# Residual and conv tiles loaded several products earlier, and the Strassen pair operands made in two steps instead of four

## The chip, the cores and the metric

The kernel runs as one program on one core of a Trainium2 chip. The metric is the device time of one execution in microseconds (us); three runs of the kernel before gave 2842.70, 2845.52 and 2847.58 us, so the median is 2845.52 us. TensorE (PE) multiplies; its weight loads are shown as PEld. VectorE (DVE), ScalarE (ACT) and GpSimd (POOL) do the elementwise work, and SyncE (SP) and POOL issue DMAs. Each engine runs its own list of instructions strictly in order, so an instruction that waits holds everything behind it on that engine.

## The reference

One layer of a decoder on 512 prompt tokens and 32 sample tokens (NT = 544 columns, held as two halves of 272):

```
proj = rmsnorm(x) @ w_in               # 2048 -> SSD group + conv group
y = rmsnorm(ssd(...) * silu(z))        # 2048 channels
u = silu(layernorm(dwconv31(...)))     # 2048 channels, the "conv half"
x = x + concat([y, u]) @ w_out         # 4096 -> 2048, the out-projection
g, v = split(dwconv3(rmsnorm(x) @ w_up))
x = x + (silu(g) * v) @ w_down         # 2048 -> 2*5504 -> 2048
return rmsnorm(x), states...
```

All of it is in float32. The kernel keeps activations transposed (channels on the 128 partitions, tokens along the row), splits every operand of a matrix product into a rounded high part and a low rest, and computes high*high + high*low + low*high, three matmuls for each 128x128 block of weights.

## The kernel before, in words

The y half of the out-projection is done early by the jobs "oy"; its result goes to DRAM (tiles `xrd`). The change lies in what follows, a stream of "products" (`items`), which one loop at the end of the function walks. Three stretches of it matter:

- **Group stage.** Eight Groups (one for output tiles t and t+8) take ten of the sixteen u tiles, with a Strassen-like scheme: seven products of five blocks each (15 matmuls) instead of eight. A Group reads five weight tiles `wr`; two of them are sums of two weight blocks, which are made by a plain load (SP, L1180) and a second load that accumulates onto it (POOL, L1182). The buffers are five in number, so the tile of the next Group is loaded when the same tile of this Group has been used up. DVE makes the sum `ws` of several of them (L1192, L1196).
- **Plain stage.** Sixteen Plain products (36 matmuls each) take the last six u tiles (`Uh`, `Ul`), one output tile each, in the order 0, 8, 1, 9, ...
- **Up stage.** 43 Groups of the up-projection, seven products of eight blocks (24 matmuls), in pairs of operands `T_t`.

Before a product can run, ACT rounds its weights (`sh`, L1205) and DVE makes the rest (`sl`, L1214), both two products ahead. After it, `evac` adds the PSUM result into the residual tile `xres`: L1253 to L1266 in the group stage, L1300 in the Plain stage. The loop makes, for product q: the ACT part for q+2, the evac of q-1, the tasks hung on q with `at_item`, the DVE part for q+2, the sums, and then the matmuls. So all of these stand in this order on DVE's and ACT's lists.

The residual tile of an output tile is x (load L1073 on SP, from `in_xT`) plus the y half (L1076 on POOL, an accumulating load of `xrd`). The six u tiles of the Plain stage come back from DRAM (`ur`, L1274) and are split into `Uh` on ACT and `Ul` on DVE (L1106, L1107). In the Plain stage the evac also makes `xs` (ACT, L1302) and a square `sq` (L1304), which POOL adds up (L1308). From each two tiles xs[k], xs[k+8] `prep_pair` makes the seven operands of the up stage in four steps, `first`, the pair of q, `second` and `third`; each step is an ACT cast (`Ta`, `Th`) followed by a DVE subtraction (`Ta` low, `Tl`), and the last two begin with DVE differences `tr` (L1126, L1127, L1132, L1133).

Of the kernel before, what the change touches and what calls it, by code (L numbers as in the profile page):

```python
# [8 lines left out]
F32 = mybir.dt.float32  # L9
F32R = mybir.dt.float32r  # L10
AF = mybir.ActivationFunctionType
ALU = mybir.AluOpType
# [18 lines left out]
def hymba_step_kernel(ctx: ExitStack, tc: tile.TileContext, a: dict):  # L31
    nc = tc.nc
    V, G, S, T, Y = nc.vector, nc.gpsimd, nc.scalar, nc.tensor, nc.sync
# [24 lines left out]
    def nm(p):  # L58
        cnt[0] += 1
        return f"{p}{cnt[0]}"  # L60

    def slot(p, shape=None, dt=F32, side=False):
        return (Cur.side if side else slots).tile(shape or [128, 2, NH], dt, tag="s", name=nm(p))
# [14 lines left out]
    def flat(t):  # L78
        return t.rearrange("p h x -> p (h x)")
# [188 lines left out]
    with tc.manual_schedule():  # L268
        win, wout, wup, wdn = a["w_in"], a["w_out"], a["w_up"], a["w_down"]

        def in_srcs(t):
            return [(win[t, :, i * 512:(i + 1) * 512], 4) for i in range(4)]
# [14 lines left out]
        st = [in_srcs(j) for j in (J_XBC + 16, J_XBC + 20, J_DT)]  # L287
# [778 lines left out]
        xres, xs, T_t = {}, {}, {}  # L1066
# [4 lines left out]
        def load_xr(t):  # L1071
            xres[t] = slot("xres")
            Y.dma_start(out=flat(xres[t]), in_=a["xT"][t])  # L1073

        def add_xr(t):
            G.dma_start(out=flat(xres[t]), in_=xr_dram[t], accum_op=ALU.add)  # L1076
# [28 lines left out]
        def split_into(h, l, src):  # L1105
            S.copy(h, src)  # L1106
            V.tensor_tensor(l, src, h.bitcast(F32), ALU.subtract)  # L1107

        tr = {}

        def prep_pair(T, k, p, q):

            def pair(src, ms):
                h, l = slot("Th", dt=F32R), slot("Tl", dt=F32R)
                split_into(h, l, src)
                for i, m in enumerate(ms):
                    T[m, k] = (h[:, i, :], l[:, i, :])

            def first():
                t = slot("Ta", dt=F32R)  # L1120
                split_into(t[:, 0, :], t[:, 1, :], p()[:, 0, :])
                T[0, k] = (t[:, 0, :], t[:, 1, :])

            def second():
                r = tr[k] = slot("tr")
                V.tensor_tensor(r[:, 1, :], p()[:, 0, :], p()[:, 1, :], ALU.subtract)  # L1126
                V.scalar_tensor_tensor(r[:, 0, :], r[:, 1, :], -1.0, q()[:, 1, :], ALU.mult, ALU.subtract)  # L1127
                pair(r, (2, 3))

            def third():  # L1130
                r, s = tr.pop(k), slot("tr")
                V.tensor_tensor(s[:, 0, :], q()[:, 1, :], p()[:, 1, :], ALU.subtract)  # L1132
                V.scalar_tensor_tensor(s[:, 1, :], r[:, 0, :], -1.0, q()[:, 0, :], ALU.mult, ALU.subtract)  # L1133
                pair(s, (4, 6))
            return first, lambda: pair(q(), (1, 5)), second, third
# [15 lines left out]
        def at_item(q, fn):  # L1151
            tasks.setdefault(q, []).append(fn)
# [88 lines left out]
        def block_evac(t):  # L1241

            w = []

            def f(m, o):
                x, y = xres[t], xres[t + 8]
                if m == 0:
                    w[:] = [slot("pd")]
                p = w[0]
                if m == 0:  # L1250
                    S.copy(p[:, 0, :], o)
                elif m == 1:
                    V.tensor_tensor(x[:, 0, :], o, x[:, 0, :], ALU.add)  # L1253
                    V.tensor_tensor(x[:, 0, :], x[:, 0, :], p[:, 0, :], ALU.add)
                elif m == 2:
                    V.tensor_tensor(p[:, 0, :], o, p[:, 0, :], ALU.add)  # L1256
                elif m == 3:
                    V.tensor_tensor(p[:, 1, :], o, p[:, 0, :], ALU.add)
                    V.tensor_tensor(x[:, 1, :], x[:, 1, :], p[:, 1, :], ALU.add)
                elif m == 4:  # L1260
                    V.tensor_tensor(p, o.unsqueeze(1).to_broadcast([128, 2, NH]), p, ALU.add)
                    V.tensor_tensor(y, y, p, ALU.subtract)
                elif m == 5:
                    V.tensor_tensor(x[:, 1, :], o, x[:, 1, :], ALU.add)
                else:
                    V.scalar_tensor_tensor(y[:, 0, :], o, -1.0, y[:, 0, :], ALU.mult, ALU.add)  # L1266
            return f


        Uh, Ul, ur = {}, {}, {}  # L1270

        def u_load(t):
            ur[t] = slot("ur")
            Y.dma_start(out=flat(ur[t]), in_=un_dram[t])  # L1274

        def u_split(t):
            Uh[t], Ul[t] = slot("Uh", dt=F32R), slot("Ul", dt=F32R)
            split_into(Uh[t], Ul[t], ur.pop(t))

        for i in range(8):  # L1280
            lo, hi = (wout[t, :, 2048 + UP * 128:4096] for t in (i, i + 8))
            q = len(items)
            Group(lo, hi, NU, T_u, block_evac(i))
            if i:
                at_item(q - 5, lambda i=i: load_xr(i))
                at_item(q - 2, lambda i=i: add_xr(i))
                at_item(q - 2, lambda i=i: load_xr(i + 8))
                at_item(q + 1, lambda i=i: add_xr(i + 8))
        for t in range(UP):
            at_item(28 + 4 * t, lambda t=t: u_load(t))  # L1290
            at_item(30 + 4 * t, lambda t=t: u_split(t))

        def out_evac(i):
# [19 lines left out]
        q = len(items)  # L1313
        for i in range(16):
            Plain(wout[OT[i], :, 2048:2048 + UP * 128], UP, lambda k: (Uh[k], Ul[k]), out_evac(i))
        for k in range(8):
            st = prep_pair(T_t, k, lambda k=k: xs[k], lambda k=k: xs[k + 8])
            for f, d in zip(st, (2, 2, 3, 3)):
                at_item(q + 2 * k + d, f)
            at_item(q + 2 * k + 3, lambda k=k: (xs.pop(k), xs.pop(k + 8)))  # L1320

        fstate, fcw = [], None

# [138 lines left out]
        for c, (n, pn) in enumerate(DOWN):  # L1462
            q = len(items)
# [234 lines left out]
```

## Time and profile before

| | |
|---|---|
| median of three runs | 2845.52 us |
| the profiled execution: time, and its span from first to last instruction | 2846.82 us, 2845.1 us |
| PE busy, share of the span | 2779.6 us, 98% |
| DVE busy | 2161.8 us, 76% |
| ACT busy | 1234.5 us, 43% |
| POOL busy | 906.8 us, 32% |
| mean granted clock of TensorE over the span | 0.991 |
| chain of work that ended last, by engine | PE 47%, DVE 1% |

Busy time of PE counts overlapping, pipelined matmuls, so 98% does not mean that it runs at its peak: the number of matmuls in a stretch tells its pace. In the page's row of 40 slices (71 us each) PE shows 9 nearly everywhere, and 8 in the three slices from 1209 to 1423 us, which hold most of the stages named above. The waits of PE in the whole span add up to some 50 us. TensorE's clock is granted at one of two levels; a clock of 0.90 in a stretch means that it ran at the lower one for a fifth of it.

### The profile page before, as it was taken

The page shows a single profiled execution, that of the slowest core. Times are in us where ns is not written, and L with a number is a line of the kernel's source. Part 1 is how long each engine was busy: PE and PEld are TensorE (multiplying, and loading weights), DVE is VectorE, ACT ScalarE, POOL GpSimd, SP SyncE. Part 2 cuts the span into 40 slices and gives each one's busy share as a digit, 9 for nine tenths or more (in the row PEclk, how much of TensorE's full clock was granted, in tenths as well). Part 3 has the DMA queues.
Part 4 walks back from the last instruction along what each step waited for, and adds up shares of the span by engine and source line. Part 5 has one row for each costly group of instructions (what it writes and reads, how often), then busy time and mean ns, then how long its engine had stood idle before and what let it go on. Part 6 is the DMA issues. An engine that isn't in the chain of part 4 may idle for free. (4 is left out here: it accounts for less than half of the span.)

```text
span 2845.1 us, 55518 instructions
## 1 busy us (share of the span) xinstructions
PE 2779.6 (98%) x22094; PEld 2749.9 (97%) x22094; DVE 2161.8 (76%) x3314; ACT 1234.5 (43%) x1827; POOL 906.8 (32%) x938
## 2 busy tenths in 40 slices
PE   8999999999999999988899999999999999999997
PEld 8999999999999999988799999999999999999997
DVE  7576665777787776666788888888888887778775
ACT  6545444333333324334444444444444443344344
POOL 5567667667666644311200000000000000100103
PEclk9999999999999999999999999999999999999999
DMA  4243244333333344586467776777776776765761
GB/s 168 84 132 100 91 144 136 102 99 105 104 98 98 93 135 130 156 216 173 122 179 184 191 195 186 192 188 189 195 191 184 197 192 207 173 182 160 176 184 64
DMA packets 197252, 433.50 MB, mean 152 GB/s; under 512 B 38400, under 2 KB 43136, under 8 KB 196992
## 3 DMA queue, kind: packets, MB, share of 16 engines
q1 hardware_dynamic: 175392, 362.57, 40.7%
q0 software_dynamic: 21600, 67.38, 13.5%
q8 instruction: 173, 2.83, 0.4%
q14 instruction: 87, 0.71, 0.1%
HBM read 385.78 MB, written 44.08 MB: 151 GB/s over the span
## 5 line engine op out<-in xcount | busy, mean ns | idle before, releaser
L1233 PE MATMUL st<-Th,sl 128*128 128x272 f32 x2880 | 835.9, 290 | 18.4 <-DVE sl L1214 18.4
L1230 PE MATMUL st<-Th,sh 128*128 128x272 f32 x2880 | 834.6, 290 | 1.0 <-ACT sh L1205 1.0
L1231 PE MATMUL st<-Tl,sh 128*128 128x272 f32 x2880 | 833.8, 290 | 0.0
L119 POOL TENSOR_TENSOR wl<-raw,wh 128x512 fp32r<-128x512 f32 x336 | 447.6, 1336 | 424.5 <-ACT wh L118 366.4
L1205 ACT CAST sh<-wr 128x1024 fp32r<-128x1024 f32 (+3 forms) x399 | 369.1, 926 | 464.2 <-PE st L1231 349.6
L1233 PEld LDWEIGHTS st<-Th,sl 128*128 128x128 f32 x2880 | 545.0, 189 | 21.2 <-DVE sl L1214 21.2
L1230 PEld LDWEIGHTS st<-Th,sh 128*128 128x128 f32 x2880 | 545.3, 189 | 1.4 <-ACT sh L1205 1.4
L1231 PEld LDWEIGHTS st<-Tl,sh 128*128 128x128 f32 x2880 | 545.0, 189 | 0.0
L229 PE MATMUL mm<-xh,wh 128*128 128x272 f32 x2304 | 483.2, 291 | 7.3 <-ACT xh L313 7.3
L229 PE MATMUL mm<-xl,wh 128*128 128x272 f32 x2304 | 479.2, 289 | 1.4 <-DVE xl L315 1.4
L229 PE MATMUL mm<-xh,wl 128*128 128x272 f32 x2304 | 478.5, 289 | 0.0
L1214 DVE TENSOR_TENSOR sl<-wr,sh 128x1024 fp32r<-128x1024 f32 (+3 forms) x399 | 427.4, 1071 | 56.0 <-ACT sh L1205 55.9
L118 ACT CAST wh<-raw 128x512 fp32r<-128x512 f32 x352 | 216.0, 616 | 433.6 <-PE mm L229 335.2
L229 PEld LDWEIGHTS mm<-xh,wh 128*128 128x128 f32 x2304 | 368.0, 188 | 16.0 <-ACT xh L313 7.3
L229 PEld LDWEIGHTS mm<-xl,wh 128*128 128x128 f32 x2304 | 365.5, 188 | 2.4 <-DVE xl L315 2.4
L229 PEld LDWEIGHTS mm<-xh,wl 128*128 128x128 f32 x2304 | 365.2, 188 | 0.0
L1182 POOL DMA_DIRECT2D wr<-in_w_up x86 | 74.9, 871 | 836.0 <-DVE pu L1348 390.7
L940 DVE SCALAR_TENSOR_TENSOR ax<-w,cfw,ax 128x512 f32<-128x512 f32 x448 | 304.2, 751 | 7.1 <-ACT ax L916 7.1
L1205 ACT CAST sh<-ws 128x1024 fp32r<-128x1024 f32 (+2 forms) x134 | 128.7, 961 | 314.3 <-DVE ws L1192 162.2
L1214 DVE TENSOR_TENSOR sl<-ws,sh 128x1024 fp32r<-128x1024 f32 (+2 forms) x134 | 149.2, 1114 | 36.2 <-ACT sh L1205 26.6
L1230 PE MATMUL st<-Ta,sh 128*128 128x272 f32 x480 | 138.7, 289 | 8.0 <-ACT Ta L1106 7.4
L1182 POOL DMA_DIRECT2D wr<-in_w_down x32 | 27.8, 869 | 368.9 <-DVE pd L1256 129.2
(327 smaller groups left out, 4663.0 us busy)
## 6 DMA issues: line engine op xcount, KB each, us to landing
wr<-in_w_up SPq DMA_DIRECT2D x215, 512.0 KB, 4.8
raw<-in_w_in SPq DMA_DIRECT2D x292, 256.0 KB, 3.1
wr<-in_w_up POOLq DMA_DIRECT2D x86, 512.0 KB, 8.0
wr<-in_w_down SPq DMA_DIRECT2D x96, 384.0 KB, 3.4
raw<-in_w_out SPq DMA_DIRECT2D x64, 256.0 KB, 2.9
wr<-in_w_out SPq DMA_DIRECT2D x40, 320.0 KB, 4.8
wr<-in_w_down POOLq DMA_DIRECT2D x32, 384.0 KB, 5.4
ad<-ra SPq DMA_DIRECT2D x43, 272.0 KB, 8.0
```

The lines of the kernel that those rows point to most:

```text
L118: S.copy(h[:, :n], r[:, :n])
L119: (cur["wl"] or eng).tensor_tensor(l[:, :n], r[:, :n], h[:, :n].bitcast(F32), ALU.subtract)
L229: T.matmul(o, lhsT=w[:, c], rhs=x[:, hf, :], start=first, stop=last)
L940: V.scalar_tensor_tensor(p, w[:, i:i + 512], wt(i), p, ALU.mult, ALU.add)
L1182: G.dma_start(out=t, in_=more, accum_op=ALU.add)
L1205: S.copy(h, src)
L1214: V.tensor_tensor(l, src, h.bitcast(F32), ALU.subtract)
L1230: T.matmul(outs[0], lhsT=h[:, c], rhs=xh_, start=k == 0, stop=False)
L1231: T.matmul(outs[0], lhsT=h[:, c], rhs=xl_, start=False, stop=False)
L1233: T.matmul(outs[0], lhsT=l[:, c], rhs=xh_, start=False, stop=k == o.K - 1)
```

## The change

Two parts. The loads of the residual tile are hung on earlier products: x for tile i 12 instead of 5 products ahead of its Group, its accumulating load 8 instead of 2 ahead; for tile i+8 9 instead of 2 ahead, and 5 ahead instead of 1 behind. The u tiles are loaded 6 instead of 2 products ahead of their split. And a new helper, `prep_two`, makes the operands of the first seven pairs: in step a all DVE differences and all four ACT casts, in step b, one product later, all four DVE subtractions. Step a stands one product later than `first` did. The last pair keeps `prep_pair`, its four steps spread over four products.

```
+        def prep_two(T, k, p, q):
+            hs = []
+            def high(t, src):
+                S.copy(t, src)
+                return t
+            def a():
+                r, s, t = slot("tr"), slot("tr"), slot("Ta", dt=F32R)
+                V.tensor_tensor(r[:, 1, :], p()[:, 0, :], p()[:, 1, :], ALU.subtract)
+                V.scalar_tensor_tensor(r[:, 0, :], r[:, 1, :], -1.0, q()[:, 1, :], ALU.mult, ALU.subtract)
+                V.tensor_tensor(s[:, 0, :], q()[:, 1, :], p()[:, 1, :], ALU.subtract)
+                V.scalar_tensor_tensor(s[:, 1, :], r[:, 0, :], -1.0, q()[:, 0, :], ALU.mult, ALU.subtract)
+                high(t[:, 0, :], p()[:, 0, :])
+                T[0, k] = (t[:, 0, :], t[:, 1, :])
+                for src, ms in ((q(), (1, 5)), (r, (2, 3)), (s, (4, 6))):
+                    hs.append((src, high(slot("Th", dt=F32R), src), ms))
+            def b():
+                h, l = T[0, k]
+                V.tensor_tensor(l, p()[:, 0, :], h.bitcast(F32), ALU.subtract)
+                while hs:
+                    src, h, ms = hs.pop(0)
+                    l = slot("Tl", dt=F32R)
+                    V.tensor_tensor(l, src, h.bitcast(F32), ALU.subtract)
+                    for i, m in enumerate(ms):
+                        T[m, k] = (h[:, i, :], l[:, i, :])
+            return a, b
...
             if i:
-                at_item(q - 5, lambda i=i: load_xr(i))
-                at_item(q - 2, lambda i=i: add_xr(i))
-                at_item(q - 2, lambda i=i: load_xr(i + 8))
-                at_item(q + 1, lambda i=i: add_xr(i + 8))
+                at_item(max(q - 12, 0), lambda i=i: load_xr(i))
+                at_item(max(q - 8, 2), lambda i=i: add_xr(i))
+                at_item(max(q - 9, 1), lambda i=i: load_xr(i + 8))
+                at_item(max(q - 5, 3), lambda i=i: add_xr(i + 8))
         for t in range(UP):
-            at_item(28 + 4 * t, lambda t=t: u_load(t))
+            at_item(24 + 4 * t, lambda t=t: u_load(t))
             at_item(30 + 4 * t, lambda t=t: u_split(t))
...
-            st = prep_pair(T_t, k, lambda k=k: xs[k], lambda k=k: xs[k + 8])
-            for f, d in zip(st, (2, 2, 3, 3)):
+            p, p8 = lambda k=k: xs[k], lambda k=k: xs[k + 8]
+            if k < 7:
+                st = list(zip(prep_two(T_t, k, p, p8), (3, 4)))
+            else:
+                st = list(zip(prep_pair(T_t, k, p, p8), (2, 3, 4, 5)))
+            for f, d in st:
                 at_item(q + 2 * k + d, f)
-            at_item(q + 2 * k + 3, lambda k=k: (xs.pop(k), xs.pop(k + 8)))
+            at_item(q + 2 * k + d, lambda k=k: (xs.pop(k), xs.pop(k + 8)))
```

No instruction is added or taken away on any engine; lines behind the new helper move down by 30 to 34.

SP's list at the start of the group stage, before: `wr` are weight tiles, `xres` residual tiles, `xrd` the store of a y half.

```order
L1180 DMA wr_14655<-in_w_out 128x640
L1180 DMA wr_14683<-in_w_out 128x640
L1073 DMA xres_14706<-in_xT 128x544
L1180 DMA wr_14710<-in_w_out 128x640
L1180 DMA wr_14713<-in_w_out 128x640
L180 DMA xrd_170<-oy_14633 128x544
L1180 DMA wr_14760<-in_w_out 128x640
L1073 DMA xres_14783<-in_xT 128x544
```

The same place now:

```order
L1180 DMA wr_14655<-in_w_out 128x640
L1073 DMA xres_14659<-in_xT 128x544
L1073 DMA xres_14683<-in_xT 128x544
L1180 DMA wr_14687<-in_w_out 128x640
L1073 DMA xres_14711<-in_xT 128x544
L1180 DMA wr_14715<-in_w_out 128x640
L1180 DMA wr_14718<-in_w_out 128x640
L180 DMA xrd_170<-oy_14633 128x544
```

Three residual loads now stand within the first weight loads, where one stood; from there on the distance stays.

POOL's list of accumulating loads at the same place, before:

```order
L1182 DMA wr_14683<-in_w_out 128x640
L1182 DMA wr_14713<-in_w_out 128x640
L1076 DMA xres_14706<-xrd_156 128x544
L1076 DMA xres_14783<-xrd_164 128x544
L1182 DMA wr_14856<-in_w_out 128x640
```

And now:

```order
L1182 DMA wr_14687<-in_w_out 128x640
L1076 DMA xres_14659<-xrd_156 128x544
L1182 DMA wr_14718<-in_w_out 128x640
L1076 DMA xres_14683<-xrd_164 128x544
L1076 DMA xres_14711<-xrd_157 128x544
```

A residual add now stands ahead of every second weight accumulation, where both weight accumulations of a Group stood ahead of both adds.

DVE's list for two Plain products, before (the operands of pair 5: `Ta`, `Tl`, `tr`):

```order
L1107 TENSOR_TENSOR Ta_16796<-xs_16726,Ta_16796 128x272
L1107 TENSOR_TENSOR Tl_16800<-xs_16792,Th_16799 128x544
L1214 TENSOR_TENSOR sl_16803<-wr_16495,sh_16787 128x768
L1300 TENSOR_TENSOR xres_15581<-st_16808,xres_15581 128x272
L1300 TENSOR_TENSOR xres_15581<-st_16809,xres_15581 128x272
L1126 TENSOR_TENSOR tr_16856<-xs_16726 128x272
L1127 SCALAR_TENSOR_TENSOR tr_16856<-tr_16856,xs_16792 128x272
L1107 TENSOR_TENSOR Tl_16860<-tr_16856,Th_16859 128x544
L1132 TENSOR_TENSOR tr_16863<-xs_16792,xs_16726 128x272
L1133 SCALAR_TENSOR_TENSOR tr_16863<-tr_16856,xs_16792 128x272
L1107 TENSOR_TENSOR Tl_16867<-tr_16863,Th_16866 128x544
L1214 TENSOR_TENSOR sl_16870<-wr_16554,sh_16847 128x768
```

The same pair now (L1290 and L1294 are the subtractions of step b):

```order
L1279 TENSOR_TENSOR tr_16849<-xs_16719 128x272
L1280 SCALAR_TENSOR_TENSOR tr_16849<-tr_16849,xs_16785 128x272
L1281 TENSOR_TENSOR tr_16850<-xs_16785,xs_16719 128x272
L1282 SCALAR_TENSOR_TENSOR tr_16850<-tr_16849,xs_16785 128x272
L1214 TENSOR_TENSOR sl_16863<-wr_16547,sh_16840 128x768
L1330 TENSOR_TENSOR xres_15486<-st_16867,xres_15486 128x272
L1330 TENSOR_TENSOR xres_15486<-st_16868,xres_15486 128x272
L1290 TENSOR_TENSOR Ta_16851<-xs_16719,Ta_16851 128x272
L1294 TENSOR_TENSOR Tl_16916<-xs_16785,Th_16857 128x544
L1294 TENSOR_TENSOR Tl_16918<-tr_16849,Th_16859 128x544
L1294 TENSOR_TENSOR Tl_16920<-tr_16850,Th_16861 128x544
L1214 TENSOR_TENSOR sl_16922<-wr_16613,sh_16906 128x1024
```

The four differences have come together in one product, and the four subtractions in the next, behind a product's evac and weight split.

## Rows read from the trace of the kernel before

**Rows 1.** Windows: us, busy (count) PE, PEld, DVE, ACT, POOL; clock, DMA share, GB/s.

```profile
1192.00:1325.00 133.00, 115.17 (x842) 112.85 (x843) 91.79 (x151) 45.61 (x72) 24.55 (x28) 0.94 0.85 210
1325.00:1418.00 93.00, 81.48 (x580) 79.57 (x579) 65.10 (x100) 44.41 (x72) 19.44 (x15) 0.93 0.45 127
1418.00:1457.50 39.50, 31.75 (x224) 30.80 (x223) 31.15 (x44) 15.98 (x23) 3.11 (x3) 0.87 0.50 140
1500.00:2300.00 800.00, 800.00 (x6354) 800.00 (x6353) 695.33 (x1023) 382.24 (x490) 66.12 (x76) 1.00 0.73 191
```

**Rows 2.** Waits of PE in the three stages: total us, times, longest.

```profile
PE st L1233 <- DVE sl L1214: 16.9, 8, 5.0
...
PE st L229 <- DVE xres L1300: 11.5, 6, 2.8
...
PE st L1230 <- ACT Ta L1106: 7.4, 1, 7.4
```

**Rows 3.** Waits of DVE, 1190 to 1325 us.

```profile
DVE xres L1253 <- DMA xres<-xrd: 17.1, 4, 6.0
...
DVE Ul L1107 <- ACT Uh L1106: 11.0, 5, 5.5
```

**Rows 4.** Timelines around one stall: start, length, instruction, [idle before <-releaser].

```profile
1239.02 0.59 SPq L1073 DMA_DIRECT2D xres<-in_xT  x1
...
1254.11 1.17 POOL L1076 DMA_DIRECT2D xres<-xrd  x1
...
1262.27 0.44 DVE L1253 TENSOR_TENSOR xres<-st,xres 128x272 f32<-128x272 f32 x1 [5.96 <-DMA xres<-xrd]
...
1263.81 0.82 DVE L1214 TENSOR_TENSOR sl<-wr,sh 128x640 fp32r<-128x640 f32 x1
...
1264.68 0.59 PE L1233 MATMUL st<-Th,sl 128*128 128x272 f32 x1 [3.96 <-DVE sl L1214]
```

**Rows 5.** DMA issues, 1192 to 1325 us: count, KB, median us to landing.

```profile
wr<-in_w_out SPq DMA_DIRECT2D x35, 320.0 KB, 4.5
wr<-in_w_out POOLq DMA_DIRECT2D x14, 320.0 KB, 5.9
xres<-in_xT SPq DMA_DIRECT2D x14, 272.0 KB, 5.5
xres<-xrd POOLq DMA_DIRECT2D x14, 272.0 KB, 7.4
```

**Rows 6.** Windows: ten microseconds at the start of the group stage.

```profile
1200.00:1210.00 10.00, 10.00 (x81) 10.00 (x80) 8.22 (x13) 4.20 (x7) 3.48 (x4) 1.00 1.02 253
```

**Rows 7.** Timeline of DVE, from a weight sum to the next Group's third split.

```profile
1206.29 0.82 DVE L1192 TENSOR_TENSOR ws<-wr,wr 128x640 f32<-128x640 f32 x1 [0.74 <-DMA wr<-in_w_out]
...
1208.73 0.82 DVE L1214 TENSOR_TENSOR sl<-wr,sh 128x640 fp32r<-128x640 f32 x1
```

**Rows 8.** Timeline of DVE, two Plain products and their pair.

```profile
1358.03 0.95 DVE L1214 TENSOR_TENSOR sl<-wr,sh 128x768 fp32r<-128x768 f32 x1
...
1361.36 1.47 DVE L1107 TENSOR_TENSOR Ta<-xs,Ta 128x272 fp32r<-128x272 f32 x1 [1.68 <-ACT Ta L1106]
...
1366.93 1.52 DVE L1107 TENSOR_TENSOR Tl<-tr,Th 128x544 fp32r<-128x544 f32 x1 [1.08 <-ACT Th L1106]
...
1369.86 0.73 DVE L1107 TENSOR_TENSOR Tl<-tr,Th 128x544 fp32r<-128x544 f32 x1 [0.71 <-ACT Th L1106]
1370.51 0.95 DVE L1214 TENSOR_TENSOR sl<-wr,sh 128x768 fp32r<-128x768 f32 x1
```

**Rows 9.** Timeline of POOL in the same stretch.

```profile
1361.16 1.37 POOL L1308 TENSOR_TENSOR sq<-sq,sq 128x544 f32<-128x544 f32 x1 [5.77 <-ACT sq L1304]
```

**Rows 10.** Timeline of DVE at the start of the up stage.

```profile
1424.02 1.22 DVE L1192 TENSOR_TENSOR ws<-wr,wr 128x1024 f32<-128x1024 f32 x1
1425.15 0.78 DVE L1300 TENSOR_TENSOR xres<-st,xres 128x272 f32<-128x272 f32 x2
1427.91 0.44 DVE L1107 TENSOR_TENSOR Ta<-xs,Ta 128x272 fp32r<-128x272 f32 x1 [1.97 <-ACT Ta L1106]
```

## The prediction

> **What bounds the kernel now.** I read the windows by stage first, because PE shows 98% busy and that says little: the count of matmuls tells its pace. In the undisturbed up stage 6354 matmuls take 800 us, so one takes 0.1259 us at a granted clock of 1.00 [rows 1]. At that pace the 842 matmuls of the group stage need 106.0 us and take 133.0, the 580 of the Plain stage need 73.0 and take 93.0, the 224 at the start of the up stage need 28.2 and take 39.5 [rows 1]. So PE loses 27.0 + 20.0 + 11.3 = 58.3 us here, and no edit to these stages can bring more than that; elsewhere nothing is changed.
>
> Then the waits of PE, stage by stage: 16.9 us on DVE's weight split `sl`, 11.5 on the Plain evac L1300 (it frees the PSUM bank), 7.4 on the cast `Ta` [rows 2]. The rest of the 58.3 us goes with the clock, whose mean is 0.94, 0.93 and 0.87 in these windows: it falls to the lower level after some of the stalls, and comes back [rows 1].
>
> Last, what DVE waits for. In the group stage it is the residual's accumulating load, 17.1 us in four waits, and the u split, 11.0 us in five [rows 3]. One stall read through: x is issued at 1239.02, the add at 1254.11, the evac L1253 waits 5.96 us for it until 1262.27; the split `sl`, finished long before as far as its inputs go, stands behind it on DVE and starts at 1263.81, and PE comes back at 1264.68 after 3.96 us [rows 4].
>
> **Part 1: earlier loads (group stage).** The same 14 residual tiles and 6 u tiles are loaded, with the same instructions on SP, POOL, ACT and DVE; only their places move. A residual add is issued 8 products ahead of its Group instead of 2, and is used two products into the Group. At full pace a product of 15 matmuls takes 15 x 0.1259 = 1.89 us, so it has 10 x 1.89 = 18.9 us until it is used, and its median landing is 7.4 [rows 1, 5]. x has 4 products, 7.6 us, until its add is issued, against a landing of 5.5 [rows 5]. The u tile gets 6 products, 11.3 us. So these two waits of DVE should go, 28.1 us of DVE time in all.
>
> What is late next is the weight pair that the first sum L1192 reads. Its buffer is free when the third split of the Group is done; then come the plain load (4.5 us), the accumulation on POOL, landed 5.9 us after its issue [rows 5], with 0.7 us allowed for the hand-over, a part of POOL's 1.17 us for an issue [rows 4], and from the sum to the end of the next Group's third split 1208.73 + 0.82 - 1206.29 = 3.3 us [rows 7]. That round is 14.4 us; PE needs 105 x 0.1259 = 13.2 us for a Group; before, a Group took 133 / 8 = 16.6. Already without a residual wait the sum had to wait 0.74 us for that load [rows 7]. And the landings will not get shorter: the stage moves 210 GB/s at a DMA share of 0.85 over 133 us [rows 1], the same bytes in less time come near the 253 GB/s at a share of 1.02 of the busiest ten microseconds [rows 6]. I take 15.0 us a Group for seven Groups and 13.2 for the first, 118.2 us, a gain of 15 us. The ends: 27.0 us if PE gets its full pace; and a loss of 10 us if the adds, now between the two weight accumulations on POOL's list, lengthen each accumulation to the adds' own 7.4 us (1.5 us, eight Groups, 12 us) and PE waits for that where it waits today, less 2 us for the u tiles. 15 is nearest to the round worked out from the median landings.
>
> One rule speaks for more. The Trainium skill, page "DMA: Bandwidth & Descriptors", section "Where 436 GB/s comes from", says that loads from HBM are bound at about 358 GB/s for a core; by that the group stage's bytes would leave room, and the gain would be 27 us, which is the second rival below. No ten microseconds of these stages come near that figure; 253 is what the row shows [rows 6].
>
> **Part 2: two steps a pair (Plain stage).** No instruction is saved. Two Plain products and their pair take DVE from 1358.03 to 1370.51, 12.48 us; in it DVE waits 1.68, 1.08 and 0.71 us for ACT's casts, since each step goes DVE, ACT, DVE [rows 8]. PE needs 72 x 0.1259 = 9.07 us, so DVE is the bound. With all differences in one product and all subtractions in the next, the casts lie a product (4.5 us) ahead of their subtractions, and the three waits go: 12.48 - 3.47 = 9.0 us, level with PE. This still holds what POOL's additions cost: `Ta` takes 1.47 us while POOL runs its 1.37 us addition, and 0.44 us where none runs [rows 8 to 10]. Two of these fall in a pair. DVE and PE being level, PSUM's double buffering covers the unevenness; I allow 1 us. Step a's four casts stand on ACT ahead of the weight cast of a later product; ACT is busy 44.41 of 93 us, so they hold nobody [rows 1]. The stage goes from 93.0 to 74.0, a gain of 19 us. The ends: 20.0, all of it; and 8, if half of the 3.5 us comes back in each of the seven pairs (7 x 1.7 = 12 less); below that I see no price, since no operation and no wait is added.
>
> The Trainium skill, page "SBUF — State Buffer", section "SBUF: two separate sides", states that of a DVE operation with two inputs in SBUF and a POOL operation that reads SBUF the one that starts first holds the shared ports for its whole length. The pair above agrees: POOL started 0.2 us earlier [rows 8, 9]. By the rule a denser DVE will sometimes start first and leave the delay to POOL, and the gain would be the whole 20 us; by the rows alone, where POOL is first, it stays at 19.
>
> **Part 3: the last pair (start of the up stage).** PE stands 7.4 us at the first up product, for `Ta` of the last pair, because DVE reaches the last evac only at 1425.15 and the cast follows it [rows 2, 10]. With DVE level with PE the last evac comes about 1.2 us after the last Plain product ends (the sum L1192 of 1.22 us stands ahead of it [rows 10]). But step b of the seventh pair now stands between that evac and the last pair: four subtractions, 0.44 + 3 x 0.65 = 2.4 us (0.65 from the start of a `Tl` to the next instruction [rows 8]). From this evac DVE's list up to 1457.50 took 1457.50 - 1425.15 = 32.4 us; 2.4 us are added, and about the 1.97 us of the wait for the cast go [rows 10]. So 1.2 + 32.8 = 34.0 us instead of 39.5, where PE needs 28.2: a gain of 5.5, of which I count 5, for a wait on the spread steps. The ends: 11.3 if PE is never held, and a loss of 2.4 if nothing goes and step b is added.
>
> **The sum.** 15 + 19 + 5 = 39 us. The profiled execution took 2846.82 us, 1.7 more than its span of 2845.1, and the median of the runs is 1.3 below it; from the median, 2845.5 - 39 = 2806.5 us.
>
> **The rivals.**
> - *DMA keeps the group stage where it is.* The waits on residual and u tiles turn into waits for the weight pair, at 16.6 us a Group. For it: a DMA share that is at 0.85 over the whole stage. Against: 253 GB/s were reached. Gain 19 + 5 = 24, so 2821.5 us.
> - *Full pace everywhere.* The weight pair is in time and DVE keeps up: 27 + 20 + 8 = 55, so 2790.5 us. For it: the first Group, with its residual already there, kept the pace at 81 matmuls in 10 us [rows 6]. Against: the round of 14.4 us.
> - *DVE stays the bound of the Plain stage.* POOL's additions and the weight splits take back half of the gain, DVE is behind at the first up product, and part 3 brings nothing: 15 + 8 = 23, so 2822.5 us.
> - *Slower.* The place is POOL's list: a weight accumulation stands behind a residual add, which waits for its own load, and that one stands on SP's list behind weight loads that wait for DVE. If the round of the weight pair grows with it, each Group pays. With 24 us from parts 2 and 3 it decides the sign from (133 + 24 + 5.7 - 13.2) / 7 = 21.4 us a Group on, 7 us above the 14.4 worked out. At 22 us a Group the stage takes 167 us, 34 more: 2845.5 + 34 - 24 = 2855.5 us. Against: x has 7.6 us for a landing of 5.5.
> - *It does not do what it says.* A load that is called earlier stands behind the same waiting weight loads on SP and starts no earlier, and DVE's casts are waited for as now: no change.
>
> **How the numbers follow.** The forecast 0.61, within 2797 to 2817 us; DMA keeps the stage 0.12; full pace 0.13; DVE stays the bound 0.08; slower 0.03; no change 0.03. Five of the six cases that I name have a sign that a measurement can tell; about 0.2% (5.7 us) is what it can. So faster 0.94, within 0.2% 0.03, slower 0.03. The range: down to 2791, which holds half of the full-pace case, and up to 2826, which holds most of the two at 2822; that leaves out about 0.07 below and 0.10 above, and lies inside the ends of the three parts, which add up to a gain of 58 us (2787) and to a loss of 10 - 8 + 2.4 = 4.4 us (2850).
>
> **What would show it.** Part 1: no wait of L1253 on `xrd` and none of `Ul`; instead waits of L1192 or of the cast L1205 on `wr`, a group stage near 118 us, its GB/s near 235. Part 2: no waits of `Ta` and `Tl` on ACT, two Plain products in 9.1 us, and no wait of PE on the evac. Part 3: a single wait of PE on `Ta` or `Tl` of some 2 to 5 us, and the clock near 1.00 in all three windows. The forecast is wrong if the group stage stays above 125 us, or if PE still waits for the Plain evac.

## The result, and the profile after

The changed kernel takes 2813.5 us (median of four runs, 2811.7 to 2815.6) against 2845.7 of the kernel before (four runs beside it), a ratio of 0.9888 with a 95% interval of 0.9871 to 0.9905: 32.2 us less, where 39 were predicted. The profiled execution has a span of 2813.8 us.

The windows of the changed kernel, by stage; the columns are those of [rows 1]:

```profile
1191.40:1315.50 124.10, 113.23 (x841) 108.25 (x842) 91.89 (x150) 45.20 (x71) 24.53 (x28) 0.99 0.90 224
1315.50:1388.40 72.90, 72.90 (x578) 72.90 (x577) 64.20 (x98) 43.14 (x69) 20.87 (x15) 1.00 0.58 163
1388.40:1426.60 38.20, 33.06 (x226) 31.30 (x225) 32.61 (x47) 17.30 (x25) 3.14 (x3) 0.91 0.55 146
```

The group stage went from 133.0 to 124.1 us, the Plain stage from 93.0 to 72.9, which is PE's own pace for its matmuls, and the start of the up stage, up to its tenth product, from 39.5 to 38.2 [rows 1]. (That stretch holds nine products of 24 matmuls and eight matmuls for the sum of squares.) So the second part of the change did all that it could, the first a good half of what was predicted, the third a quarter in this execution.

What waits in the group stage now (from the waits of 1191 to 1316, all engines; total, times, longest):

```profile
...
ACT sh L1205 <- DMA wr<-in_w_out: 19.7, 8, 3.9
DVE sl L1214 <- ACT sh L1205: 17.3, 21, 2.7
...
DVE ws L1192 <- DMA wr<-in_w_out: 8.4, 4, 3.8
...
PE st L1233 <- DVE sl L1214: 6.1, 13, 1.5
PE st L1230 <- ACT sh L1205: 5.2, 5, 2.4
DVE Ul L1107 <- ACT Uh L1106: 4.7, 4, 1.9
```

The two waits for weights in the kernel before (of ACT and of DVE, 1190 to 1330):

```profile
ACT sh L1205 <- DMA wr<-in_w_out: 11.3, 5, 4.2
...
DVE ws L1192 <- DMA wr<-in_w_out: 1.3, 3, 0.7
```

DVE's wait for the residual, 17.1 us before [rows 3], is gone from the list. In its place the waits for the weights, of ACT's cast and of the first sum, have grown from 12.6 to 28.1 us. Of the u split's 11.0 us, 4.7 stay: they are waits for a cast that is issued just ahead, not for the u tile.

The landings in the same stretch (transfers, KB each, median us from issue to landing):

```profile
wr<-in_w_out SPq DMA_DIRECT2D x35, 320.0 KB, 5.2
wr<-in_w_out POOLq DMA_DIRECT2D x14, 320.0 KB, 7.2
...
```

The weight accumulation lands 7.2 us after its issue, where it took 5.9 [rows 5]. There are two in a Group: the first pair (a21 + a22) goes into the first sum L1192, the second pair (a11 + a21) is the weight of the Group's fifth product, and on DVE's list its split stands just ahead of the second sum L1196. Taken apart, on the mean of the last six Groups, the first pair's takes 5.7 us (5.8 before), the second pair's 8.3 (6.3 before). One such round, in rows of the timelines of POOL, ACT, DVE and PE (start us, length, what; in brackets the idle time before it and what ended it):

```profile
1264.57 1.17 POOL L1076 DMA_DIRECT2D xres<-xrd  x1
1267.96 0.87 POOL L1182 DMA_DIRECT2D wr<-in_w_out  x1 [2.22 <-DVE pd L1261]
...
1276.39 0.73 ACT L1205 CAST sh<-wr 128x640 fp32r<-128x640 f32 x1 [3.18 <-DMA wr<-in_w_out]
...
1277.15 0.83 DVE L1214 TENSOR_TENSOR sl<-wr,sh 128x640 fp32r<-128x640 f32 x1 [2.36 <-ACT sh L1205]
...
1278.03 0.39 PE L1233 MATMUL st<-Th,sl 128*128 128x272 f32 x1 [0.34 <-DVE sl L1214]
```

POOL issues y's residual add first, at 1264.57, then the second pair's accumulation at 1267.96; the cast waits for it until 1276.39, 8.4 us later, and split and matmul follow at once. L1196 stands behind this split on DVE. The next Group's second pair is loaded only when it is done: on SP its load follows that of a12, whose buffer L1196 is the last to read. So the distance from one L1196 to the next is the whole round. The sums of the stage (min, median and max ns, first and last start):

```profile
L1192 DVE TENSOR_TENSOR ws<-wr,wr x8: 815/824/826, 1193.0 to 1301.8; 128x640 f32<-128x640 f32 x8
L1196 DVE TENSOR_TENSOR ws<-ws,wr x8: 817/818/822, 1197.7 to 1309.3; 128x640 f32<-128x640 f32 x8
```

(1309.3 - 1197.7) / 7 = 15.9 us a Group for the second sum, (1301.8 - 1193.0) / 7 = 15.5 for the first. PE would need 13.2.

In the Plain stage, one pair on DVE, which answers to [rows 8], and POOL's addition beside it [rows 9]:

```profile
1341.08 2.14 DVE L1214 TENSOR_TENSOR sl<-wr,sh 128x768 fp32r<-128x768 f32 x1
1343.14 0.78 DVE L1330 TENSOR_TENSOR xres<-st,xres 128x272 f32<-128x272 f32 x2
1343.84 0.42 DVE L1290 TENSOR_TENSOR Ta<-xs,Ta 128x272 fp32r<-128x272 f32 x1
1344.19 0.71 DVE L1294 TENSOR_TENSOR Tl<-xs,Th 128x544 fp32r<-128x544 f32 x1
1344.83 2.51 DVE L1294 TENSOR_TENSOR Tl<-tr,Th 128x544 fp32r<-128x544 f32 x2
1347.26 0.95 DVE L1214 TENSOR_TENSOR sl<-wr,sh 128x768 fp32r<-128x768 f32 x1
...
1341.04 1.36 POOL L1338 TENSOR_TENSOR sq<-sq,sq 128x544 f32<-128x544 f32 x1 [3.63 <-ACT sq L1334]
```

No instruction waits for a cast any more. The split at 1341.08 takes 2.14 us beside POOL's addition and 0.95 without one.

At the start of the up stage, on DVE, POOL and PE, where before stood [rows 10]:

```profile
1388.17 0.42 DVE L1279 TENSOR_TENSOR tr<-xs 128x272 f32<-128x272 f32 x1
...
1389.80 2.39 DVE L1214 TENSOR_TENSOR sl<-wr,sh 128x1024 fp32r<-128x1024 f32 x1
1392.11 1.21 DVE L1192 TENSOR_TENSOR ws<-wr,wr 128x1024 f32<-128x1024 f32 x1
1393.25 0.78 DVE L1330 TENSOR_TENSOR xres<-st,xres 128x272 f32<-128x272 f32 x2
1393.94 0.43 DVE L1290 TENSOR_TENSOR Ta<-xs,Ta 128x272 fp32r<-128x272 f32 x1
...
1389.72 1.38 POOL L1338 TENSOR_TENSOR sq<-sq,sq 128x544 f32<-128x544 f32 x1 [3.89 <-ACT sq L1334]
...
1394.43 0.60 PE L1231 MATMUL st<-Ta,sh 128*128 128x272 f32 x1 [3.44 <-DVE Ta L1290]
```

The last Plain product ends at 1388.4. The last evac comes at 1393.25, 4.8 us later, since four differences of pair 6, a weight split that POOL's addition doubles, and the first sum stand ahead of it; the first subtraction of step b follows, and PE waits 3.4 us for it. Behind this stall the clock is at its lower level for 6.8 us. The stall is longer in this execution than in others: in the six other kernels with the same steps (runs 2, 3, 5, 6, 7 and 9 below) the last evac comes 2.8 to 3.3 us after the last Plain product, and PE waits 1.4 to 1.9 us.

### The profile page after: what moved, and what is told of

The parts are those of the page before. It is cut to its first block, busy times and chain, and to the rows that moved or that the text cites. A ratio compares the mean times of both kernels' runs of the same rounds, so it can differ in the third digit from the quotient of the medians.

```text
span 2813.8 us, 55523 instructions
## 1 busy us (share of the span) xinstructions
PE 2770.0 (98%) x22094; PEld 2738.6 (97%) x22094; DVE 2158.6 (77%) x3314; ACT 1234.0 (44%) x1827; POOL 907.4 (32%) x938
## 4 chain that ended last, share of the span: by engine, by line
PE 91%; DMA 4%; DVE 3%; issue 1%; ACT 0%; POOL 0%; SPq 0%; POOLq 0%; DVEq 0%; ACTq 0%
PE mm L229 37%; PE st L1233 14%; PE st L1231 14%; PE st L1230 14%; PE st L229 8%; DMA wr<-in_w_out 3%; PE ax L229 2%; DVE sl L1214 1%; DMA x<-in_xT 1%; PE ax L658 1%; PE ax L597 0%; DVE Tl L1294 0%; DVE o L499 0%; PE ax L662 0%; DVE xl L315 0%
## 5 line engine op out<-in xcount | busy, mean ns | idle before, releaser
L1233 PEld LDWEIGHTS st<-Th,sl 128*128 128x128 f32 x2880 | 542.6, 188 | 12.7 <-DVE sl L1214 12.5
L229 PEld LDWEIGHTS mm<-xh,wh 128*128 128x128 f32 x2304 | 367.8, 188 | 15.9 <-ACT xh L313 7.1
```

Source lines behind the costliest of these rows:

```text
L229: T.matmul(o, lhsT=w[:, c], rhs=x[:, hf, :], start=first, stop=last)
L1233: T.matmul(outs[0], lhsT=l[:, c], rhs=xh_, start=False, stop=k == o.K - 1)
```

## The experiments

Three stretches of each kernel's profiled execution, and its times. "Group" is from the first product of the group stage to the first Plain product, "up" from the first up product to the end of the span, and the ratio is to the kernel before.

| kernel | group us | Plain us | up us | median us | ratio, interval |
|---|---|---|---|---|---|
| before | 132.9 | 92.9 | 1427.3 | 2845.7 | 1 |
| changed | 124.0 | 72.9 | 1425.4 | 2813.5 | 0.9888, 0.9871 to 0.9905 |
| 1 loads only | 122.3 | 92.8 | 1426.5 | 2835.2 | 0.9963, 0.9950 to 0.9975 |
| 2 pairs only | 130.0 | 72.9 | 1424.3 | 2823.8 | 0.9920, 0.9906 to 0.9933 |
| 3 y behind | 119.5 | 72.9 | 1424.4 | 2810.1 | 0.9876, 0.9863 to 0.9890 |
| 4 last sooner | 123.3 | 73.3 | 1424.6 | 2814.0 | 0.9887, 0.9873 to 0.9900 |
| 5 no y add | 115.9 | 72.9 | 1422.6 | 2804.6 | 0.9859, 0.9844 to 0.9873 |
| 6 POOL adds | 124.5 | 72.9 | 1422.9 | 2818.4 | 0.9904, 0.9889 to 0.9919 |
| 7 six buffers, 74 slots | 112.1 | 72.9 | 1423.7 | 2815.7 | 0.9896, 0.9880 to 0.9913 |
| 8 sums on PE | 120.9 | 72.9 | 1421.8 | 2809.6 | 0.9880, 0.9864 to 0.9897 |
| 9 sixth buffer | 113.2 | 72.9 | 1422.7 | 2802.8 | 0.9853, 0.9839 to 0.9866 |
| 10 sixth + sums on PE | 112.2 | 72.9 | 1421.1 | 2800.1 | 0.9845, 0.9832 to 0.9859 |
| 11 the same + last sooner | 112.1 | 72.9 | 1422.4 | 2799.7 | 0.9843, 0.9829 to 0.9856 |

How far a stretch differs between executions can be read from it: four kernels have the changed kernel's group stage (changed, 1, 4, 8), at 120.9 to 124.0 us, mean 122.6; two have the old one (before, 2), mean 131.4.

**1 and 2: each part alone.** The kernel before with the earlier loads, and the kernel before with the two steps. The edits are the two halves of the change.

> The kernel before with the earlier residual and u loads alone. If the parts are independent: the group stage (first stream product to first Plain product) takes 124 us as in the changed kernel, the Plain stage stays at 93, the start of the up stage near 39.5, so 2845.7 - 8.8 = about 2837 us. Rival, the parts hang together (the later stages of the changed kernel gained because their loads and buffers came earlier): the Plain stage falls below 90 us here too, and the time is under 2834.

> The kernel before with the pair operands in two steps alone. Independent parts: group stage 133 us as before, Plain stage 73, start of the up stage about 38, so 2845.7 - 21.5 = about 2824 us. Rival, hang together: the Plain stage stays above 78 us, since DVE comes into it late from the group stage, and the time is above 2830.

The windows of the Plain stage, of the first and of the second:

```profile
1313.80:1406.60 92.80, 81.41 (x579) 79.50 (x577) 64.93 (x101) 44.22 (x71) 19.46 (x15) 0.93 0.45 128
```

```profile
1322.00:1394.90 72.90, 72.90 (x578) 72.90 (x577) 64.11 (x100) 45.40 (x73) 23.09 (x16) 1.00 0.59 163
```

2835.2 and 2823.8 us: 10.9 and 22.3 us less than the 2846.1 beside them, 33.2 together, against 32.2 for the whole. The parts are independent, and DVE's work in the Plain stage is the same 64 to 65 us busy in both: the two steps save no work, they end waits.

**3: y's add behind the second weight accumulation.**

```diff
-                at_item(max(q - 5, 3), lambda i=i: add_xr(i + 8))
+                at_item(max(q - 4, 3), lambda i=i: add_xr(i + 8))
```

On POOL's list this exchanges two neighbours, six times, and nothing else.

> The changed kernel with one exchange on POOL's list: the residual add of y stands behind the second weight accumulation (a11+a21) instead of ahead of it. Theory, the round of this pair bounds the stage (sum L1196 to sum L1196 takes 15.95 us on the mean of six Groups; its accumulation takes 8.2 us where it took 6.1 in the kernel before) because the y add is issued just ahead of it: the accumulation falls to about 7 us, the round to about 14.8, seven Groups give some 8 us, group stage 116, 2805.5 us. Rival, the DMA engines' throughput (busy share 0.90 over the stage) is the bound and order is nothing: group stage 122 to 126 us, 2813 us.

The window, the landings, and POOL's timeline around one Group:

```profile
1192.00:1311.50 119.50, 111.26 (x840) 109.16 (x841) 92.40 (x152) 45.71 (x71) 24.52 (x28) 0.97 0.92 234
```

```profile
wr<-in_w_out POOLq DMA_DIRECT2D x14, 320.0 KB, 6.0
```

```profile
1264.52 0.89 POOL L1182 DMA_DIRECT2D wr<-in_w_out  x1 [1.98 <-DVE xres L1262]
1265.13 1.18 POOL L1076 DMA_DIRECT2D xres<-xrd  x1
...
1270.44 0.73 ACT L1205 CAST sh<-wr 128x640 fp32r<-128x640 f32 x1 [1.14 <-DMA wr<-in_w_out]
```

Two of its waits in the group stage, of DVE (1191 to 1312) and of ACT (1192 to 1311.5):

```profile
DVE ws L1192 <- DMA wr<-in_w_out: 12.7, 5, 3.3
...
ACT sh L1205 <- DMA wr<-in_w_out: 7.1, 5, 2.1
```

From issue to cast 5.9 us instead of 8.4, and on the mean of the last six Groups the second pair's accumulation takes 6.0 us instead of 8.3. That is larger than the scatter: in the changed kernel and in runs 1, 4 and 8, which have y's add ahead, the mean is 7.4 to 8.3; in the kernel before and in runs 2, 3 and 9, where it is not ahead, 6.0 to 6.3. So it is shown that y's add, ahead of it, lengthens this accumulation. What that costs the stage is less sure: it gains 3.1 us against the mean of 122.6, not the 8 expected, and the four executions behind that mean lie 3.1 us apart. The first pair is late next: ACT's wait for weights falls from 19.7 to 7.1 us, that of the first sum rises from 8.4 to 12.7, and from L1192 to L1192 it is (1298.6 - 1193.6) / 7 = 15.0 us. In the time the gain isn't told apart, since the intervals of 0.9876 and 0.9888 overlap.

**4: the last two pairs a product sooner.** `(3, 4)` becomes `(2, 3)` for pair 6, and `(2, 3, 4, 5)` becomes `(1, 2, 3, 4)` for pair 7.

> The changed kernel with the last two pairs' steps one product sooner (pair 6 at 2 and 3 instead of 3 and 4, pair 7 at 1 to 4 instead of 2 to 5). Theory, the stall of 3.72 us at the first up product comes from what stands on DVE's list ahead of the first low part of pair 6 (four differences, a weight split, a weight sum): it goes below 1 us, the clock stays high where it fell for 6.8 us, and the start of the up stage takes about 32 us instead of 38.2: 2808 us. Rival, DVE's whole list from the last Plain products on is the bound, and the wait only moves to later products: start of the up stage 37 to 39 us, 2813 us.

The longest waits of PE in the 38.2 us from the first up product on:

```profile
PE st L1233 <- DVE sl L1214: 3.7, 5, 1.7
PE st L1230 <- ACT Th L1106: 1.4, 1, 1.4
PE st L1231 <- DVE Ta L1107: 1.0, 1, 1.0
```

The rival holds: the wait for pair 6 (3.4 us on `Ta` L1290) is gone, and one for pair 7 (1.0 us) and waits on the weight split and a cast take its place. Up to the tenth up product it is 37.4 us, against 38.2 in the changed kernel and 35.4 to 37.2 in the six others with its steps, although the clock is at 1.00 instead of 0.91. So DVE's list is the bound there, not its order; run 8 below shortens the list.

**5: no y add.** Without the call `add_xr(i + 8)` in the group stage.

> The changed kernel without the seven residual adds of the y tiles in the group stage; it leaves out the attention half of the residual for output tiles 9 to 15. Theory, bytes: the accumulating queue takes 6.05 us of all 16 DMA engines per MB in the changed kernel (41.9% of 124.1 us for 8.60 MB), so 1.95 MB less are 11.8 us, and the DMA work of the stage falls from 0.90 x 124.1 = 112 us to 100, under PE's 106: group stage 109 to 113 us, 2800 us. Rival, order alone (the y add ahead of the second weight accumulation): as with the exchange, 119.5 us, 2809 us.

The window:

```profile
1192.00:1307.90 115.90, 109.45 (x841) 106.49 (x842) 91.61 (x150) 45.17 (x71) 18.41 (x21) 1.00 0.87 223
```

115.9 us lies between the two expectations. The second pair's accumulation takes 5.9 us, as with the exchange; the 3.6 us beyond run 3 are put down to the bytes, but a stage differs by nearly as much between executions. PE still loses 10 us at a DMA share of 0.87, so the bytes alone are not the bound.

**6: POOL adds the residual.** In place of the accumulating DMA a plain load into `xa` and an addition:

```diff
-            G.dma_start(out=flat(xres[t]), in_=xr_dram[t], accum_op=ALU.add)
+            G.tensor_tensor(xres[t], xres[t], xa.pop(t), ALU.add)
```

> The changed kernel with the 14 residual adds done by POOL: a plain load of the attention half into a tile of its own and an addition on POOL instead of an accumulating DMA. Plain loads take 3.07 us of the 16 engines per MB against 6.05, so the DMA work falls by 11.6 us as in the run without the y adds, with nothing left out. Theory, bytes bound the stage: 112 to 115 us, 2803 us. Rival, DVE becomes the bound: 14 POOL additions that each stretch a DVE instruction by up to 1.2 us and hold POOL's own list: group stage 118 us or more, 2808 us or later.

```profile
1192.20:1316.70 124.50, 112.28 (x840) 108.39 (x841) 105.09 (x150) 45.07 (x71) 31.65 (x28) 0.99 0.82 224
```

```profile
1253.07 2.60 DVE L1262 TENSOR_TENSOR xres<-xres,pd 128x544 f32<-128x544 f32 x1
...
1253.39 1.68 POOL L1308 TENSOR_TENSOR xres<-xres,xa 128x544 f32<-128x544 f32 x1
```

In its window, and in one piece of DVE's and POOL's timelines, the rival shows: the DMA share falls from 0.90 to 0.82, but the same 150 instructions keep DVE busy for 105.1 us instead of 91.9, and PE's waits on the split `sl` rise from 6.1 to 8.5 us. L1262 takes 2.60 us beside POOL's addition, 0.72 without. That DVE and not POOL's longer list holds the stage is argued from these rows, not shown.

**7: six raw buffers, two slots fewer.** `free = [6]`, `bufs=6`, `NSLOT = 74`, with run 3's edit.

> The changed kernel with y's add behind the second weight accumulation and six raw weight buffers instead of five (two of 76 slots are given up for it). Theory, the round of a buffer (load, accumulation, sums) is what is late: each load starts one buffer earlier, group stage 111 to 113 us, where the DMA work (0.92 x 119.5 = 110 us) is next: 2802 us. Rival, the DMA engines are the bound already: 117 to 120 us, 2809 us.

```profile
1208.40:1320.50 112.10, 108.56 (x841) 106.38 (x841) 91.30 (x150) 45.20 (x71) 24.50 (x28) 1.00 0.96 248
```

The window shows the stage as expected, and its start 17 us late. The whole of that is lost early: PE is 0.5 us behind the changed kernel at 361 us of the span and 16.9 us behind at 493, long before the group stage. The missing slots are the likely cause, but the run changes slots and buffers together. A result on the round, and a miss on the time.

**9: a sixth buffer without that cost.** For the 40 loads of the group stage every sixth goes into a tile of 640 columns, in room that is free once the earlier weight pool is closed; run 3's edit is in it too.

```diff
+                if n_load[0] % 6 == 5 and n_load[0] < 40:
+                    t = w6.tile([128, 640], F32, tag="r6", bufs=1, name=nm("wr"))
...
+                if n_load[0] == 40:
+                    free[0] -= 1
...
+        w6 = swap("w6", bufs=1, side="right")
+        issue(1)
```

> The changed kernel with y's add behind the second weight accumulation and a sixth raw weight buffer for the 40 loads of the group stage, opened in the room that is free once the earlier weight pool has gone, so that no slot is given up. Theory, the round of a buffer bounds the stage: group stage 111 to 114 us as in the run with 74 slots (112.1), without what that run lost ahead of the stage: 2813.5 - 12 = 2801.5 us. Rival, that run had its short group stage only because it came to it 16 us late, with its loads done ahead: here 117 to 120 us, 2808 us.

Its windows of the group stage and of the 38.2 us from the first up product on:

```profile
1192.20:1305.30 113.10, 108.98 (x840) 107.66 (x841) 91.36 (x151) 45.31 (x71) 24.49 (x28) 0.98 0.96 245
1378.20:1416.40 38.20, 33.99 (x240) 32.11 (x240) 33.41 (x48) 17.55 (x24) 2.11 (x3) 0.96 0.57 156
```

The theory holds, 113.1 us and 2802.8: 6.4 us less in the stage than run 3, and the three other kernels with six buffers (7, 10 and 11) take 112.1 to 112.2. No landing got shorter (weight accumulations 6.3 us, plain weight loads 5.0 in the median, against 6.0 and 4.8 in run 3); each load only starts a buffer earlier. So the round of a buffer was the bound, with the engines' share at 0.92 in run 3, and not their throughput, since the share could still go to 0.96.

**8, 10 and 11: the last three sums of squares on PE.** POOL adds only up to the twelfth tile; the last four tiles go into the sum over partitions on PE.

```diff
-                elif i < 15:
+                elif i < 12:
...
-                    spawn(rsqrt_gen([fst["acc"], sq], setr("r2")), 3)
+                    fst.setdefault("late", [fst["acc"]]).append(sq)
+                    if i == 15:
+                        spawn(rsqrt_gen(fst["late"], setr("r2")), 3)
```

Run 8 is this on the changed kernel, run 10 on run 9, run 11 has run 4's edit besides.

> The changed kernel with the last three of POOL's additions of squares taken away: the three tiles go into the sum over partitions on PE instead (six fp32 matmuls more, in a stretch where PE waits). Theory, DVE's list is the bound of the start of the up stage and POOL's additions stretch it (a weight split 2.39 us instead of 1.21): some 3 us less from the last Plain product to the tenth up product, 35.5 us instead of 38.2, 2810.5 us. Rival, the differences of pair 6 and the weight split ahead of the last evac alone make the stall: first stall still over 3 us, 2813 us.

> As the run before it, with the last three sums of squares on PE. If the two gains add up: group stage 111 to 114 us, start of the up stage 2 to 3.5 us shorter than in the changed kernel, about 2798.5 us. Rival, they don't (the Plain stage or the up stage's start takes back what the group stage gives): 2802 us or more.

> As the run before it, with the steps of the last two pairs one product sooner. Theory, with POOL's additions gone DVE has room for the steps in the Plain stage: 2 us less than the run before, 2796.5 us. Rival, DVE's list is as long and the wait only moves, as in the run with the sooner steps alone (0.7 us): the same time within 1 us.

Run 8 on DVE around the last evac, run 10's window from the first up product on, and PE's matmuls for the sum over partitions in run 9 and in run 10 (count, min, median and max ns, first and last start):

```profile
1384.23 1.22 DVE L1214 TENSOR_TENSOR sl<-wr,sh 128x1024 fp32r<-128x1024 f32 x1
1385.36 1.22 DVE L1192 TENSOR_TENSOR ws<-wr,wr 128x1024 f32<-128x1024 f32 x1
1386.49 0.78 DVE L1330 TENSOR_TENSOR xres<-st,xres 128x272 f32<-128x272 f32 x2
```

```profile
1376.80:1412.00 35.20, 33.69 (x241) 31.74 (x240) 29.16 (x43) 15.20 (x20) 1.73 (x2) 1.00 0.61 165
```

```profile
L239 PE MATMUL ax<-sq,ones x8: 392/392/393, 1395.8 to 1397.4; 128*128 128x272 f32 x8
```

```profile
L239 PE MATMUL ax<-sq,ones x20: 392/392/393, 1390.7 to 1395.0; 128*128 128x272 f32 x20
```

The split takes 1.22 us instead of 2.39, and the last evac comes 0.6 us after the last Plain product (its end is at 1385.9) instead of 4.8. PE's first wait there is 0.6 us, so the rival of run 8, a first stall of over 3 us, is out. Run 10's 35.2 us and run 9's 38.2 hold nearly the same number of matmuls, but twelve of run 10's are the added sums, so its window ends at an earlier place among the products. Up to the tenth up product run 10 takes 34.2 us and run 9 35.7: 1.5 us less, and at the end of the span it is 1.6 (1421.1 against 1422.7). The twelve matmuls take PE 12 x 0.23 = 2.8 us (0.23 us from one start to the next), so by estimate DVE's shorter list gives some 4 us and PE pays back the larger part. Runs 8 and 9 each have the larger part of their gain elsewhere, so this edit's time is not told apart. Run 11 equals run 10 within 0.5 us, as its rival said. Run 10 beats both kernels: 0.9845 with an interval that ends at 0.9859, below the 0.9871 at which that of the changed kernel begins.

## Why the prediction was right in its sign and 7 us short

- **Plain stage, 19 predicted, 19.9 measured.** Right, and by the steps named: the three waits for casts are gone, and PE sets the pace with no wait on the evac. One reading was off: the text took DVE to be level with PE, from the 9.0 us of one pair, but DVE has 64.2 us of work in 72.9, as the 65.1 us of the whole stage before [rows 1] could have told. Then to the place where a rule was weighed. The Trainium skill, page "SBUF — State Buffer", section "SBUF: two separate sides", lets the one of DVE and POOL that starts first hold the shared ports; a denser DVE would then sometimes have left the delay to POOL. In the rows above POOL starts 0.04 us ahead, its addition keeps 1.36 us, and DVE's split takes 2.14 instead of 0.95, which agrees with the rule; but in run 6 L1262 starts 0.32 us ahead of POOL and takes 2.60 us all the same, which does not. The whole gain came all the same, out of DVE's slack of 9 us.
- **Group stage, 15 predicted, 8.8 measured** (means of 131.4 and 122.6). The step that failed is the weight pair's round: "from the median landings", 5.9 us for the accumulation, worked out for the first sum. (The first pair's buffer is freed by the Group's fourth split, not the third as the text has it; the row that it read, 1208.73, is the right one.) The second pair's accumulation, whose split L1196 stands behind, went to 8.3 us, because the y add moved ahead of it on POOL's list, and its round to 15.9 us. The text had this as its lower end ("the adds, now between the two weight accumulations on POOL's list, lengthen each accumulation") and priced it at 1.5 us each; it came to 2.0 on every second pair. With the order put right (run 3) the first pair's round is the 15.0 us that was predicted, and the stage 119.5, against 118.2.
- **Start of the up stage, 5 predicted, 3.2 measured** (mean of seven kernels with the new steps, 1423.7 us from the first up product to the end of the span, against 1426.9 for the two with the old ones). The step that failed is "the last evac comes about 1.2 us after the last Plain product ends": it came 4.8 us after it (2.8 to 3.3 in the six other kernels with these steps), since step a of pair 6 and a split that POOL stretched by 1.2 us stood there too, and only step b had been counted. The single wait of PE was there, 3.4 us; the clock was not near 1.00 in that window, but 0.91.
- **The sum**: 8.8 + 19.9 + 3.2 = 31.9, and 32.2 measured.
- **The rivals.** That DMA keeps the group stage is refuted by runs 7 and 9, which pass the same bytes in 112 to 113 us; but its mechanism, that the waits turn into waits for the weight pair, is the one that came, at 15.9 us a Group instead of 16.6. Full pace failed at that round. DVE did not stay the bound of the Plain stage. Of the Trainium skill's page "DMA: Bandwidth & Descriptors", section "Where 436 GB/s comes from", which puts the bound of loads from HBM at about 358 GB/s for a core: no run of this stage shows more than 248 on the mean, and there the share of the engines is 0.96, so their own time is the nearer limit here. For short times the rate is higher than the page's figure: in 40 slices of the stage, some 3 us each, the largest is 360 GB/s in the changed kernel and 410 in run 9. (The text's 253 is not the highest of the ten-microsecond windows either: from 1440 to 1450, in the up stage, it is 279.)
- **What was to be seen**: the residual's wait went, as said; those of `Ul` did not all go (4.7 us). The stage moved 224 GB/s, not 235, and took 124.1 us, just under the 125 above which the text would have called itself wrong.

What stays open: how much of the group stage's time the order on POOL's list costs, since run 3's gain is of the size of the scatter, and what holds the stage in run 6.

## What to carry to other kernels

A transfer that is moved earlier is also moved ahead of something: look up which transfer stands behind it in its queue, and work out the round of every buffer that this one serves, not of the one that is late today. When a stage is held by the round of a buffer, one more buffer can gain more than a new order does (6.4 against 3.1 us here), even at a DMA share of 0.92; look for the room first, since room taken from another stage may cost more than the gain. Work that is moved from one engine to another is paid there: compare two kernels at the same product, not at the same count of instructions. And a chain of steps that goes from DVE to ACT and back is sped up without saving an instruction by doing all of one engine's steps for the pair first and the other's a product later.

## What the runs showed of the hardware

- Transfers on POOL's queue, which all accumulate here, took twice as much of the DMA engines for their bytes as those on SP's, which are plain. In the changed kernel from 1191 to 1316 us POOL's queue moved 8.60 MB in 41.9% of the 16 engines' time, SP's 19.26 MB in 47.3%: 6.1 against 3.1 us per MB. No run tells the accumulation from the queue.
- An accumulation of 320 KB with two others of its queue still under way at its issue took 7.4 to 8.3 us on the mean (the second pair in the changed kernel and runs 1, 4 and 8); with one or none under way 6.0 to 6.3 us (the kernel before and runs 2, 3 and 9).
- A DVE operation with two SBUF inputs was stretched beside a POOL addition from 0.95 to 2.14 us (changed kernel) and from 0.72 to 2.60 us (run 6), in the second case although its recorded start is ahead of POOL's (1253.07 against 1253.39).
